# A hybrid decoder layer on one core: branch-weight sums formed in place in four load buffers from the head's second column group on, and a paced inverse that ends 480 matmuls from the last

## Chip, core and metric

One NeuronCore of one Trainium2 chip runs the whole layer in one launch. The metric is the device time of one execution in microseconds (us); the time before is the median of three runs. Engines are named as the profile names them: PE (TensorE matmul), PEld (its weight load), DVE (VectorE), ACT (ScalarE), POOL (GpSimd) and SP (SyncE, which here only issues DMAs, in order). `L123` is line 123 of the kernel before.

## What is computed

A decoder layer on 1024 rows of 1024 channels, float32 in and out:

```
hn   = rmsnorm(x);  proj = hn @ w_in
y_fox = forgetting_attention(fq, fk, fv, log_sigmoid(ff + bias))      # 8 heads of 128
y_gdn = gated_delta_rule(l2norm(q), l2norm(k), v, g, beta)            # q,k,v = silu(causal conv), chunks of 64
        # each chunk solves (I + A) sol = [v*beta, k*beta*exp(gc)], A strictly lower triangular 64x64
y = sigmoid(gate_fox) * (y_fox @ w_branch_fox) + sigmoid(gate_gdn) * (y_gdn @ w_branch_gdn)
h = x + y @ w_out
h = h + (silu(u_gate) * u_val) @ w_down,   u = causal conv(rmsnorm(h) @ w_up)
out = rmsnorm(h)
```

## The kernel before

Every float32 product is made of three matmuls on split operands (a high part in fp32r, copied by ACT, and the rest, subtracted by DVE or POOL: `split`, L106 and L107). Large products are done by Strassen's scheme in Winograd's form on 512-wide quarters: seven products of 12 matmuls in place of eight, with sums of quarters formed ahead (`weight_sums` for weights, `block_sums` for activations). The stages follow each other on PE in program order, since PE's order is written by hand; the other engines' orders are laid out by the framework's scheduler ahead of the run, and each engine, SP's DMA issues among them, runs its own list strictly in order.

**The head** (`head_in`, L541 on) normalises and transposes x, and multiplies it by the token weights `w_tok` in four column groups g of 262 columns and eight row tiles t: `rows(g, t)` is 24 matmuls into one of eight PSUM banks, an ACT copy into `vev` (two buffers, L574) and a DMA `vd<-vev` (L580). The group's weights come in quarters `vwr` (L560), are split by ACT and POOL into `vwh` and `vwl`, and have two buffers. Between the rows of the groups g = 1 to 3 the program also takes steps of two other generators: `scalars` (the gates' scalars) and `prepare_merge`, called `sums` there. `block_sums` forms the activation sums t1 to t4 of the next stage (DVE L343 to L362).

`prepare_merge` (L991) works ahead for a stage 1000 us later: for both branches and k = 0 to 3, eight blocks in all, it loads two 128x1024 tiles `raw` of `w_branch` (L1001, 512 KB each, two buffers), has DVE form four sums of 128x512 from their halves (L985 to L988, `weight_sums`), and stores them to DRAM (L1006, 1 MB). The sums go into a tile `sums` of 128x2048 with one buffer, so the next block's sums wait until this block's store has landed. One step issues a block's loads, the next its sums and its store; the loop in `head_in` takes one step for each row tile from g = 1, t = 4 on.

**The projections** (`project`, L716 on) follow: `strassen` runs 32 jobs of 84 matmuls (L156), 2688 in all; a job loads two weight tiles `wr` (L125, three buffers), forms the weight sums `ws` on DVE (L202), operands on ACT and POOL (`oh`, `ol`), and takes its results out of PSUM with ACT (`x`, L258; `c`, L311) and DVE (L289, L300, L315). Their buffers lie in memory that the head gives back. `left` counts the matmuls still to come, and the loop at L877 on uses it to thread other work between them:

- `inverse` (L922), the triangular solve of all chunks, 124 steps, nearly all of them a pair of DVE operations (L962, L964) on up to 128x512. It starts once the heads' own work is done, at `left = begin`, and is paced by one line:

```
if (begin - left) * INVERSE_STEPS >= (begin - 340) * steps:
```

- `prepare_lead` (L1009) in the memory that the inverse gives back, a step at each multiple of 20 of `left`: it loads six `w_up` tiles (L1017), forms one set of weight sums, splits 13 quarters into `parts` (two buffers) and stores them (L1023, `lead`) for the up projection.
- `fox_first` (L1072) in the memory that `prepare_lead` gives back: its first step loads the first attention head's q, k, v and bias rows (L1042, L1065); the later ones, at each multiple of 10 of `left` below 130, scale q (L1050), split k (`kh`, `kl`) and multiply (L1104 to L1106), the first time at `left` = 100.

**The merge** (`merge_block`, L1354) later loads the stored sums in 128x512 pieces (L1361).

Of the kernel before, what the change touches and what calls it, by code (L numbers as in the profile page):

```python
# [17 lines left out]
P = 128  # L18
# [69 lines left out]
class Block:  # L88
# [452 lines left out]
    def head_in(self, blk, right):  # L541
# [3 lines left out]
        with tc.tile_pool(name="hin", bufs=1) as pool, ExitStack() as px:  # L545
# [75 lines left out]
            for g in range(1, NVG):  # L621
                w = wgroup(g, nc.gpsimd)
                take(scalars, 1)
                for t in range(NT):
                    rows(g, t, *w)
                    if g > 1 or t > 3:
                        take(sums, 1)
                    if t % 4 == 2 and g < 3:
                        sl = slice((2 * (g - 1) + t // 4) * P, (2 * (g - 1) + t // 4 + 1) * P)
                        self.block_sums(blk, whole("12", sl), whole("22", sl), sl, pool)  # L630
# [85 lines left out]
    def project(self, blk, fox_pool):  # L716
# [159 lines left out]
        with ExitStack() as ix:  # L876
            for i, _ in enumerate(self.strassen(jobs, blk, pace=3)):  # L877
# [21 lines left out]
                elif prep is None:  # L899

                    if (begin - left) * INVERSE_STEPS >= (begin - 340) * steps:
                        steps += 1
                        if not take(inv, 1):
                            ix.close()
                            prep = self.prepare_lead(ix.enter_context(tc.tile_pool(name="prep", bufs=1, reuse_waits="tile")))
# [73 lines left out]

    def weight_sums(self, pool, a11, a12, a21, a22):  # L980

        v = self.nc.vector
        t = pool.tile([P, 2048], F32, tag="sums", bufs=1, name="sums")
        s1, s2, s3, s4 = (t[:, 512 * i:512 * (i + 1)] for i in range(4))
        self.tc.keep_in_program_order(v.tensor_tensor(s1, a21, a22, ALU.add))  # L985
        v.tensor_tensor(s2, s1, a11, ALU.subtract)
        v.tensor_tensor(s3, a11, a21, ALU.subtract)
        v.tensor_tensor(s4, a12, s2, ALU.subtract)  # L988
        return t

    def prepare_merge(self, pool):  # L991

        nc, a = self.nc, self.a
        self.ms_d = [[self.dr.tile([P, 2048], F32, name=f"ms{br}{k}") for k in range(4)] for br in range(2)]
        left, right = slice(0, 512), slice(512, 1024)
        for br in range(2):
            for k in range(4):
                raws = []
                for half in range(2):
                    t = pool.tile([P, 1024], F32, tag="raw", bufs=2, name="raw")  # L1000
                    self.tc.keep_in_program_order(nc.sync.dma_start(t, a["w_branch"][KD * br + 4 * half + k]))  # L1001
                    raws.append(t)
                yield
                r0, r1 = raws
                t = self.weight_sums(pool, r0[:, left], r1[:, left], r0[:, right], r1[:, right])
                self.tc.keep_in_program_order(nc.sync.dma_start(self.ms_d[br][k], t))  # L1006
                yield

    def prepare_lead(self, pool):  # L1009
# [10 lines left out]
        def parts(j, src):  # L1020
            t = pool.tile([P, 1024], F32R, tag="parts", bufs=2, name="parts")
            self.split(t[:, left], t[:, right], src)
            nc.sync.dma_start(self.lead_d[j], t.bitcast(F32))  # L1023

        w1, w2 = (load(a["w_up"][2 * FF_ORDER[0] + i]) for i in range(2))
        yield
        t = self.weight_sums(pool, w1[:, left], w1[:, right], w2[:, left], w2[:, right])
        parts(0, w1[:, left])
        parts(1, w1[:, right])
        yield  # L1030
        for i, n in enumerate((1, 2, 0, 3)):
            parts(9 + i, t[:, 512 * n:512 * (n + 1)])
        for j in range(1, 5):
# [320 lines left out]
    def merge_block(self, pool, br, name, k, t=None):  # L1354
# [4 lines left out]
        if name[0] == "s":  # L1359
            i = int(name[1]) - 1  # L1360
            self.nc.sync.dma_start(t, self.ms_d[br][k][:, 512 * i:512 * (i + 1)])  # L1361
            return t
# [569 lines left out]
```

## Time and profile before

| quantity | value |
|---|---|
| median of 3 runs | 2057.82 us (2057.77 to 2064.13) |
| the profiled execution | 2060.05 us, span 2058.3 us |
| mean granted TensorE clock | 0.978 |
| busy PE / DVE / ACT / POOL | 94% / 71% / 52% / 47% of the span |
| head, up to the first matmul of the projections | 166.08 us |
| projections' matmuls (L156) | 166.08 to 858.2 us |

The span runs from the first to the last instruction, and the profiled execution's own time is 1.75 us longer. A busy share of 94% on PE says that most stages are bound by it, and that what is to be won lies where it stands still. The profile's page cuts the span into 40 slices of 51.5 us and gives each engine's busy share in tenths; the stretches are then looked at one by one. In the views "[4.7 <-DMA x]" behind a row is the idle time of its engine just before it and what ended it, and "waited for" rows give the total, the times and the longest.

### The profile page before, as it was taken

The numbers are of one execution on the slowest core, as the hardware profiler recorded it, in microseconds if no ns is written. First come the engines' busy times: TensorE is split into PE (matmuls) and PEld (weight loads), VectorE is DVE, ScalarE is ACT, GpSimd is POOL, SyncE is SP. The second block draws the span as 40 slices with busy tenths as digits, with TensorE's granted clock in tenths as the row PEclk, the third lists the DMA queues.
The fourth block names the chain that finished last, engine by engine and source line by source line (L and its number), as shares of the span: only waits on it lengthen the run. The fifth ranks groups of instructions, "written<-read, shape, count | busy, mean of one in ns | idle before, by whom it ended". The sixth has DMA issues, their size and how long they took to land. (4 is left out here: it accounts for less than half of the span.)

```text
span 2058.3 us, 29148 instructions
## 1 busy us (share of the span) xinstructions
PE 1924.9 (94%) x9628; PEld 1605.7 (78%) x9628; DVE 1465.4 (71%) x2514; ACT 1076.3 (52%) x2354; POOL 973.2 (47%) x818
## 2 busy tenths in 40 slices
PE   7937999999999999788999999999999999999998
PEld 6935888878887787578887788777788888877886
DVE  8925776874898977466776898667867667677535
ACT  5304777764334445466767444366655555553224
POOL 5704556555555454346765333235565665640012
PEclk9968999999999999889999999999999999999999
DMA  4473444445333348557663863565443343368654
GB/s 161 141 250 121 139 131 149 141 138 193 109 113 118 108 143 301 199 182 234 196 224 112 307 197 116 175 210 184 134 145 117 128 142 119 128 216 324 222 194 159
DMA packets 177896, 350.95 MB, mean 171 GB/s; under 512 B 50320, under 2 KB 62928, under 8 KB 176720
## 3 DMA queue, kind: packets, MB, share of 16 engines
q1 hardware_dynamic: 177600, 348.56, 50.8%
q8 instruction: 76, 1.25, 0.3%
q14 instruction: 76, 0.62, 0.1%
q10 hardware_dynamic: 144, 0.52, 0.1%
HBM read 232.79 MB, written 116.23 MB: 170 GB/s over the span
## 5 line engine op out<-in xcount | busy, mean ns | idle before, releaser
L107 POOL TENSOR_TENSOR ol<-ws,oh 128x512 fp32r<-128x512 f32 x212 | 285.5, 1350 | 235.4 <-ACT oh L106 227.6
L107 POOL TENSOR_TENSOR ol<-wr,oh 128x512 fp32r<-128x512 f32 x165 | 231.6, 1405 | 313.5 <-ACT oh L106 213.4
L106 ACT CAST oh<-ws 128x512 fp32r<-128x512 f32 x212 | 130.9, 618 | 171.8 <-PE mm L156 163.7
L106 ACT CAST oh<-wr 128x512 fp32r<-128x512 f32 x204 | 123.5, 616 | 147.2 <-PE mm L156 80.1
L202 DVE TENSOR_TENSOR ws<-wr 128x512 f32<-128x512 f32 x106 | 97.8, 922 | 142.6 <-DMA wr<-in_w_up_dram 74.2
L377 DVE SCALAR_TENSOR_TENSOR cv<-c,fw,cv 128x512 f32<-128x512 f32 (+2 forms) x176 | 127.3, 748 | 16.5 <-ACT cv L372 15.3
L156 PE MATMUL mm<-b11h,oh 128*128 128x512 f32 x216 | 85.9, 398 | 42.2 <-ACT oh L106 42.2
L377 DVE SCALAR_TENSOR_TENSOR cv<-c,cw,cv 128x511 f32<-128x511 f32 (+2 forms) x144 | 105.9, 748 | 7.3 <-ACT cv L372 5.4
L962 DVE TENSOR_TENSOR invt<-invz 128x399 f32<-128x399 f32 (+50 forms) x114 | 95.7, 856 | 0.4
L156 PE MATMUL mm<-b22h,oh 128*128 128x512 f32 x216 | 86.7, 401 | 8.5 <-ACT x L258 8.2
L258 ACT COPY x<-mm 128x512 f32<-128x512 f32 x158 | 91.9, 582 | 4.5 <-PE mm L156 4.5
L156 PE MATMUL mm<-bt1h,oh 128*128 128x512 f32 x216 | 85.2, 394 | 4.8 <-ACT x L258 4.7
L107 DVE TENSOR_TENSOR ol<-wd,oh 128x512 fp32r<-128x512 f32 x66 | 46.3, 705 | 58.0 <-ACT oh L106 58.0
L156 PE MATMUL mm<-b22l,oh 128*128 128x512 f32 x216 | 86.5, 400 | 0.0
L156 PE MATMUL mm<-b11l,oh 128*128 128x512 f32 x216 | 86.1, 399 | 0.0
L156 PE MATMUL mm<-b11h,ol 128*128 128x512 f32 x216 | 86.0, 398 | 0.1
L156 PE MATMUL mm<-b21l,oh 128*128 128x512 f32 x216 | 86.0, 398 | 0.0
L156 PE MATMUL mm<-bt4l,oh 128*128 128x512 f32 x216 | 85.7, 397 | 0.0
L156 PE MATMUL mm<-bt2l,oh 128*128 128x512 f32 x216 | 85.1, 394 | 0.3 <-DVE bt2l L107 0.3
L156 PE MATMUL mm<-b22h,ol 128*128 128x512 f32 x216 | 85.1, 394 | 0.0
L156 PE MATMUL mm<-bt1l,oh 128*128 128x512 f32 x216 | 84.9, 393 | 0.0
L156 PE MATMUL mm<-bt3l,oh 128*128 128x512 f32 x216 | 84.8, 392 | 0.0
(404 smaller groups left out, 6388.4 us busy)
## 6 DMA issues: line engine op xcount, KB each, us to landing
wr<-in_w_up_dram SPq DMA_DIRECT2D x43, 512.0 KB, 3.7
wr<-in_w_gdn_dram SPq DMA_DIRECT2D x24, 512.0 KB, 3.6
wr<-in_w_out_dram SPq DMA_DIRECT2D x24, 512.0 KB, 4.4
s<-hy SPq DMA_DIRECT2D x44, 256.0 KB, 2.9
s<-z SPq DMA_DIRECT2D x44, 256.0 KB, 3.4
wd<-in_w_down_dram SPq DMA_DIRECT2D x44, 256.0 KB, 5.9
b22h<-s SPq DMA_DIRECT2D x44, 256.0 KB, 2.8
b22l<-s SPq DMA_DIRECT2D x44, 256.0 KB, 3.3
```

Of the source, the lines that this page charges most:

```text
L106: nc.scalar.copy(hi, src)
L107: (lo_eng or nc.vector).tensor_tensor(lo, src, hi.bitcast(F32), ALU.subtract)
L156: self.nc.tensor.matmul(ps, lhs[:, sl], rhs[:, k, :], start=(first and k == 0 and i == 0), stop=(k == 3 and i == 2), skip_group_check=True)
L202: v.tensor_tensor(t, x, y, op)
L258: nc.scalar.copy(t, x)
L377: nc.vector.scalar_tensor_tensor(t[:, lo:], c[:, 512 * j + lo - s:512 * (j + 1) - s], w[:, n - 1 - s:n - s], t[:, lo:], op0=ALU.mult, op1= ...
L962: nc.vector.tensor_tensor(tv, z[:, m:n, 0:n].to_broadcast([P, r, n]), z[:, m, c0:c1].unsqueeze(2).to_broadcast([P, r, n]), ALU.mult))
```

## The change

1. `weight_sums` writes its four sums into the halves that it read (in place) and needs no `sums` tile; `raw` in `prepare_merge` has four buffers in place of two, and each of a block's two `raw` tiles is stored by a DMA of its own (512 KB) into a tile of its own.
2. The loop in `head_in` takes a step of `sums` for every row tile from g = 1, t = 0 on, four row tiles earlier.
3. The inverse's pace ends at 480 matmuls from the last in place of 340.
4. `prepare_lead` uses the sums in place too (the two plain quarters are split first), and `parts` has four buffers in place of two.
5. `merge_block` finds each sum at its new place.

```diff
-                    if g > 1 or t > 3:
-                        take(sums, 1)
+                    take(sums, 1)
...
-                    if (begin - left) * INVERSE_STEPS >= (begin - 340) * steps:
+                    if (begin - left) * INVERSE_STEPS >= (begin - 480) * steps:
...
-    def weight_sums(self, pool, a11, a12, a21, a22):
+    def weight_sums(self, a11, a12, a21, a22):
 
         v = self.nc.vector
-        t = pool.tile([P, 2048], F32, tag="sums", bufs=1, name="sums")
-        s1, s2, s3, s4 = (t[:, 512 * i:512 * (i + 1)] for i in range(4))
-        self.tc.keep_in_program_order(v.tensor_tensor(s1, a21, a22, ALU.add))
-        v.tensor_tensor(s2, s1, a11, ALU.subtract)
-        v.tensor_tensor(s3, a11, a21, ALU.subtract)
-        v.tensor_tensor(s4, a12, s2, ALU.subtract)
-        return t
+        self.tc.keep_in_program_order(v.tensor_tensor(a22, a21, a22, ALU.add))
+        v.tensor_tensor(a21, a11, a21, ALU.subtract)
+        v.tensor_tensor(a11, a22, a11, ALU.subtract)
+        v.tensor_tensor(a12, a12, a11, ALU.subtract)
...
-                    t = pool.tile([P, 1024], F32, tag="raw", bufs=2, name="raw")
+                    t = pool.tile([P, 1024], F32, tag="raw", bufs=4, name="raw")
...
-                t = self.weight_sums(pool, r0[:, left], r1[:, left], r0[:, right], r1[:, right])
-                self.tc.keep_in_program_order(nc.sync.dma_start(self.ms_d[br][k], t))
+                self.weight_sums(r0[:, left], r1[:, left], r0[:, right], r1[:, right])
+                for d, t in zip(self.ms_d[br][k], raws):
+                    self.tc.keep_in_program_order(nc.sync.dma_start(d, t))
...
-            t = pool.tile([P, 1024], F32R, tag="parts", bufs=2, name="parts")
+            t = pool.tile([P, 1024], F32R, tag="parts", bufs=4, name="parts")
...
-        t = self.weight_sums(pool, w1[:, left], w1[:, right], w2[:, left], w2[:, right])
         parts(0, w1[:, left])
         parts(1, w1[:, right])
         yield
-        for i, n in enumerate((1, 2, 0, 3)):
-            parts(9 + i, t[:, 512 * n:512 * (n + 1)])
+        self.weight_sums(w1[:, left], w1[:, right], w2[:, left], w2[:, right])
+        for j, t in enumerate((w1[:, left], w2[:, left], w2[:, right], w1[:, right])):
+            parts(9 + j, t)
...
-            i = int(name[1]) - 1
-            self.nc.sync.dma_start(t, self.ms_d[br][k][:, 512 * i:512 * (i + 1)])
+            i, j = {"s2": (0, 0), "s3": (0, 1), "s4": (1, 0), "s1": (1, 1)}[name]
+            self.nc.sync.dma_start(t, self.ms_d[br][k][i][:, 512 * j:512 * (j + 1)])
```

The lines of the kernel after lie one to three above those before. SP's list shows the head's part. Where `prepare_merge` begins, before the change, SP has (numbers behind an underscore tell buffers and DRAM tiles apart; `ms00` is block 0's store):

```order
L580 DMA vd_91<-vev_807 128x262
L1001 DMA raw_818<-in_w_branch_dram 128x1024
L1001 DMA raw_820<-in_w_branch_dram 128x1024
L580 DMA vd_91<-vev_847 128x262
L580 DMA vd_91<-vev_881 128x262
L1001 DMA raw_884<-in_w_branch_dram 128x1024
L1006 DMA ms00_810<-sums_850 128x2048
L1001 DMA raw_886<-in_w_branch_dram 128x1024
```

And with the change (`ms000` and `ms001` are block 0's two stores, `raw_692` and `raw_694` its tiles):

```order
L580 DMA vd_91<-vev_673 128x262
L998 DMA raw_692<-in_w_branch_dram 128x1024
L998 DMA raw_694<-in_w_branch_dram 128x1024
L560 DMA vwr_1329<-in_w_tok_dram 128x524
L580 DMA vd_91<-vev_721 128x262
L560 DMA vwr_1333<-in_w_tok_dram 128x524
L580 DMA vd_91<-vev_755 128x262
L998 DMA raw_758<-in_w_branch_dram 128x1024
L998 DMA raw_760<-in_w_branch_dram 128x1024
L580 DMA vd_91<-vev_809 128x262
L1004 DMA ms000_676<-raw_692 128x1024
L560 DMA vwr_1337<-in_w_tok_dram 128x524
```

The first loads stand four `vd` rows earlier, block 1's loads stand ahead of block 0's stores, and two `vwr` loads of the third group's weights now stand behind branch-weight loads.

Where the head's list ends and the projections' loads `wr` begin, SP has before the change:

```order
L1001 DMA raw_1351<-in_w_branch_dram 128x1024
L1006 DMA ms11_815<-sums_1293 128x2048
L1001 DMA raw_1353<-in_w_branch_dram 128x1024
L580 DMA vd_91<-vev_1564 128x262
L1001 DMA raw_1417<-in_w_branch_dram 128x1024
L1006 DMA ms12_816<-sums_1383 128x2048
L1001 DMA raw_1419<-in_w_branch_dram 128x1024
L1006 DMA ms13_817<-sums_1449 128x2048
L125 DMA wr_1686<-in_w_gdn_dram 128x1024
```

And with it:

```order
L998 DMA raw_1269<-in_w_branch_dram 128x1024
L580 DMA vd_91<-vev_1432 128x262
L1004 DMA ms120_688<-raw_1201 128x1024
L580 DMA vd_91<-vev_1460 128x262
L1004 DMA ms121_689<-raw_1203 128x1024
L580 DMA vd_91<-vev_1488 128x262
L1004 DMA ms130_690<-raw_1267 128x1024
L1004 DMA ms131_691<-raw_1269 128x1024
L580 DMA vd_91<-vev_1516 128x262
L580 DMA vd_91<-vev_1544 128x262
L580 DMA vd_91<-vev_1572 128x262
L125 DMA wr_1694<-in_w_gdn_dram 128x1024
```

In both, the first `wr` stands behind the last block's store; with the change three of the last group's `vd` rows stand between them, where before the last `vd` came four rows ahead of the end.

The third place is SP's list around the first attention loads (`ql`), before the change (`gzd0` to `gzd7` are the results of the last eight chunks of the projections, two a job):

```order
L774 DMA gzd2_1655<-c1_7759 128x1024
L1023 DMA lead4_7552<-parts_7741 128x1024
L1023 DMA lead5_7553<-parts_7745 128x1024
L774 DMA gzd3_1656<-c2_7869 128x1024
L1023 DMA lead6_7554<-parts_7796 128x1024
L1023 DMA lead7_7555<-parts_7800 128x1024
L1023 DMA lead8_7556<-parts_7837 128x1024
L1042 DMA ql_7846<-qd0_1637 128x1024
```

And with it:

```order
L1021 DMA lead6_7318<-parts_7544 128x1024
L1021 DMA lead7_7319<-parts_7548 128x1024
L1021 DMA lead8_7320<-parts_7593 128x1024
L125 DMA wr_7819<-in_w_gz_dram 128x1024
L125 DMA wr_7821<-in_w_gz_dram 128x1024
L1040 DMA ql_7602<-qd0_1645 128x1024
L1040 DMA kl_7604<-kd0_1653 128x1024
L1063 DMA cr_7605<-rows_620 128x1024
L1040 DMA vl_7607<-vd_91 128x8x128
L773 DMA gzd0_1661<-c1_7645 128x1024
```

The attention loads stood behind `gzd3` and stand ahead of `gzd0` now, two jobs of the projections earlier.

More of the change, by code (lines that the diff above doesn't have):

```diff
@@ L977, in inverse @@
         self.dump("yd", self.y_d)
-    def weight_sums(self, pool, a11, a12, a21, a22):
+    def weight_sums(self, a11, a12, a21, a22):
         v = self.nc.vector
-        t = pool.tile([P, 2048], F32, tag="sums", bufs=1, name="sums")
-        s1, s2, s3, s4 = (t[:, 512 * i:512 * (i + 1)] for i in range(4))
-        self.tc.keep_in_program_order(v.tensor_tensor(s1, a21, a22, ALU.add))
-        v.tensor_tensor(s2, s1, a11, ALU.subtract)
-        v.tensor_tensor(s3, a11, a21, ALU.subtract)
-        v.tensor_tensor(s4, a12, s2, ALU.subtract)
-        return t
+        self.tc.keep_in_program_order(v.tensor_tensor(a22, a21, a22, ALU.add))
+        v.tensor_tensor(a21, a11, a21, ALU.subtract)
+        v.tensor_tensor(a11, a22, a11, ALU.subtract)
+        v.tensor_tensor(a12, a12, a11, ALU.subtract)
     def prepare_merge(self, pool):
         nc, a = self.nc, self.a
-        self.ms_d = [[self.dr.tile([P, 2048], F32, name=f"ms{br}{k}") for k in range(4)] for br in range(2)]
+        self.ms_d = [[[self.dr.tile([P, 1024], F32, name=f"ms{br}{k}{i}") for i in range(2)] for k in range(4)]
+                     for br in range(2)]
         left, right = slice(0, 512), slice(512, 1024)
```

## The prediction

> **What bounds it now.** I read the page's slices first, to find where PE stands still, then the waits, windows and rows of those places.
>
> ```profile
> span 2058.3 us, 29148 instructions
> PE   7937999999999999788999999999999999999998
> PEclk9968999999999999889999999999999999999999
> ```
>
> PE is full nearly everywhere. The third to fifth digits (103 to 206 us: 3, then 7) and the two at 823 to 926 us (7, 8) are the low ones, and the granted clock falls at the same places. The list of what PE waited for has two long rows, the first from 40 to 260 us, the second from 450 to 960 us; the windows and rows below belong to the first.
>
> ```profile
> PE mm L156 <- ACT oh L106: 42.2, 1, 42.2
> PE ms L1104 <- ACT kh L106: 7.3, 1, 7.3
> ...
> 124.00:166.00 42.00, 0.00 (x0) 0.00 (x0) 11.07 (x16) 2.66 (x8) 0.00 (x0) 0.53 0.69 245
> 160.00:175.00 15.00, 8.79 (x29) 6.68 (x30) 4.42 (x5) 5.55 (x12) 7.62 (x7) 0.65 0.59 211
> ...
> 107.54 0.69 DVE L988 TENSOR_TENSOR sums<-raw,sums 128x512 f32<-128x512 f32 x1
> 135.57 0.69 DVE L987 TENSOR_TENSOR sums<-raw 128x512 f32<-128x512 f32 x1 [6.68 <-DMA ms<-sums]
> 138.12 0.69 DVE L988 TENSOR_TENSOR sums<-raw,sums 128x512 f32<-128x512 f32 x1
> 145.65 0.69 DVE L987 TENSOR_TENSOR sums<-raw 128x512 f32<-128x512 f32 x1 [6.83 <-DMA ms<-sums]
> 157.96 0.32 SPq L1006 DMA_DIRECT2D ms<-sums  x1
> 161.84 1.28 SPq L125 DMA_DIRECT2D wr<-in_w_gdn_dram  x3
> 166.08 0.80 PE L156 MATMUL mm<-b11h,oh 128*128 128x512 f32 x1 [42.15 <-ACT oh L106]
> ```
>
> For 42 us PE does nothing because the first `wr` load stands on SP behind the last branch-weight store. That store is the end of a chain in which each block waits for the store of the one before: 145.65 - 135.57 = 10.1 us a block, of which about 7 are the wait for the store, with DVE, ACT and POOL nearly idle. From the last store's issue to the first matmul pass 166.08 - 157.96 = 8.1 us.
>
> **Term 1, the head.** With four tiles and no `sums`, two blocks are in flight, and a tile's round is load, sums, store, next load. Their lengths, from the DMA view of 96 to 162 us (GB/s in 40 slices; issues with KB each, median us from issue to landing):
>
> ```profile
> GB/s 0 7 273 439 328 373 13 111 258 417 251 295 225 27 121 313 432 397 232 75 86 375 441 397 222 0 119 271 442 402 201 0 112 390 432 338 0 0 397 238
> DMA packets 4897, 15.59 MB, mean 236 GB/s; under 512 B 544, under 2 KB 2464, under 8 KB 4000
> ...
> ms<-sums SPq DMA_DIRECT2D x7, 1024.0 KB, 6.3
> raw<-in_w_branch_dram SPq DMA_DIRECT2D x12, 512.0 KB, 5.4
> ...
> wr<-in_w_gdn_dram SPq DMA_DIRECT2D x1, 512.0 KB, 3.5
> ...
> 99.24 0.69 DVE L362 TENSOR_TENSOR tt<-tt,b21l 128x512 f32<-128x512 f32 x1
> ```
>
> A half-size store has no row; it lies between the 3.5 of the quickest half-size transfer and the 6.3 of the whole one. I take 6.3, since two halves leave together and move the same bytes. The round is 5.4 + 2.9 (four sums of 0.69 with their gaps, the last begun at 138.12 where the first could begin at 135.57, less a wait of 0.4) + 6.3 + 0.7 (two SP issues ahead) = 15.3 us for two blocks. The start: SP now loads blocks 0 and 1 ahead of any store, and DVE's list has block 2's sums around the last `block_sums` operation, the row of 99.24 before. Three sums more stand ahead of that row than before, so block 2 ends at 99.9 + 3 x 1.2 (between 0.69 and the 1.7 of sums beside a busy POOL) = 103.5, where it ended at 108.2 before; block 3, in the other two tiles, 3.5 later, at 107. Blocks 5 and 7 follow a round each: 107 + 2 x 15.3 = 137.6. The tail of 8.1 stays: three `vd` rows stand there now, but they are short beside it and one of them waits as `wr` did for the store. PE resumes at **145.7 instead of 166.1: 20.4 us less.** The bytes allow it: four blocks' loads and six blocks' stores, 10.5 MB, and 1.8 of `vd`, in 34 us are 360 GB/s, above the mean of 236, which holds pauses, and below the 380 of the row at 780 us.
>
> ```profile
> 780.00:790.00 10.00, 10.00 (x46) 8.29 (x45) 8.62 (x10) 5.50 (x10) 5.19 (x5) 1.00 1.02 380
> ```
>
> Bounds: rounds of 3.5 + 2.9 + 3.5 give 107 + 19.8 + 8.1 = 135 (31 less); rounds of 20, as slow a block as now, give 155 (11 less). PE idles for over 10 us in all of them, so the half clock of its first matmuls stays. The Trainium skill, "DMA: Bandwidth & Descriptors", section "Bandwidth", asks for transfers of 1 MiB or more, so it speaks against halving the stores. By its 341 GB/s at 1 MB against 138 at 64 KB a 512 KB store would be the poorer, and as an estimate from that page 1 to 2 us a block would go, 6 to 12 us of this term. The `raw` rows speak for less: 512 KB land in 5.4 where 1 MB needs 6.3, two at a time.
>
> ```profile
> 94.14 1.33 POOL L107 TENSOR_TENSOR vwl<-vwr,vwh 128x524 fp32r<-128x524 f32 x1
> 98.20 0.28 PE L570 MATMUL ms<-vwh,b21h 128*128 128x262 f32 x1
> ```
>
> The third group's last `vwl` split stands behind the last `block_sums` split on POOL now; it ends near 107 instead of 95.5, while PE reaches that group's later rows from 98.2 on. PE may lose up to 6 us there. It costs nothing: the wait until 145.7 lies behind it.
>
> **Term 2, the attention inputs.** At 821.6 us PE has 100 matmuls left and waits for the first attention head's k.
>
> ```profile
> 816.59 5.09 SPq L1023 DMA_DIRECT2D lead<-parts  x3
> 821.73 0.42 SPq L1042 DMA_DIRECT2D ql<-qd  x1
> ...
> 827.01 1.06 ACT L1050 ACTIVATE qh<-ql 128x1024 fp32r<-128x1024 f32 x1 [5.40 <-DMA ql<-qd]
> ...
> 773.16 3.01 SPq L1017 DMA_DIRECT2D raw<-in_w_up_dram x4
> ...
> ACT parts L106 <- DMA lead<-parts: 4.0, 5, 2.5
> ...
> 828.87 0.58 PE L1104 MATMUL ms<-kh,qh 128*128 128x256 f32 x1 [7.30 <-ACT kh L106]
> 511.90:755.40 243.50, 239.79 (x1053) 196.88 (x1052) 218.92 (x317) 95.18 (x166) 127.53 (x91) 1.00 0.34 114
> 820.00:830.00 10.00, 2.15 (x8) 1.24 (x7) 2.61 (x3) 3.81 (x6) 2.37 (x2) 0.79 0.87 284
> 830.00:840.00 10.00, 9.50 (x33) 7.93 (x34) 2.94 (x14) 4.91 (x12) 5.32 (x5) 0.70 0.03 8
> ```
>
> The loads stand behind the last `lead` store, and `prepare_lead` runs from 773.2 to 821.7, as it starts when the inverse is out of its memory. Ending the inverse 140 matmuls earlier moves all that by 140 x 0.2277 (239.79 / 1053, the row of 511.90) = 31.9 us against PE; the loads and splits need 828.87 - 821.73 = 7.1 of them, which leaves 24 us. The four `parts` add the 4.0 of ACT's waits. Gone: 7.3 of waiting, 1.0 of the next, and the clock: 0.3 of the 9.5 busy us at 830 to 840 and 0.5 of the 1.1 before, 3.4. **11.7 us less.** Bounds 8 (a remainder at POOL, where `kl` and `cd` now stand ahead of nine operand splits) and 12.
>
> **Term 3, the denser inverse.** Its window is the row of 511.90 above, in which 124 steps end at 340 matmuls from the last. DVE's groups in it (busy, mean ns | idle before):
>
> ```profile
> L962 DVE TENSOR_TENSOR invt<-invz 128x399 f32<-128x399 f32 (+50 forms) x114 | 95.7, 856 | 0.4
> L964 DVE TENSOR_TENSOR invz<-invz,invt 128x399 f32<-128x399 f32 (+50 forms) x114 | 61.0, 547 | 1.7
> ...
> L202 DVE TENSOR_TENSOR ws<-ws,wr 128x512 f32<-128x512 f32 x13 | 13.2, 1019 | 6.8 <-POOL ol L107 6.7
> L300 DVE TENSOR_TENSOR c<-mm,x 128x512 f32<-128x512 f32 x13 | 8.9, 687 | 10.5 <-ACT x L258 10.5
> ```
>
> 1053 matmuls pass for 114 pairs, 9.2 each; 124 steps put the start near 340 + 124 x 9.3 = 1490 left, and the new end makes the stretch (1490 - 480) / (1490 - 340) = 0.88 as long, 214 us. DVE is busy for 218.9 us; the groups add up to 235 (they overlap), 156.7 of it the inverse, so 145.8 busy us are its own and 73 the projections', 0.30 a us. Afterwards: 145.8 + 0.30 x 214 = 210 of 214 us, 98% where it was 90%. PE loses 3.7 us in this window now (243.5 - 239.79). At best DVE's idle time, which is waiting for work, simply goes, and PE loses nothing more. At worst all 24.6 us of it stay, shortened to 21.6, on top: 210 + 21.6 - 214 = 17.6 more. I take **4 us more**, twice the present loss, the nearest row.
>
> The merge's 128x512 loads keep their bytes and their stage; I cost them at 0, within 1 either way, hidden by their four to six buffers.
>
> **Sum.** -20.4 - 11.7 + 4.0 = -28.1, from the profiled execution's 2060.05: 2032. That execution is 2.2 above the median, so against 2057.82 the forecast is **2030 us**. PE sets the pace between these places, so what is won in the head arrives at the end.
>
> **Rivals.**
> - *The chain keeps up with the rows.* With short transfers PE resumes at 135 or before: 31 less, 2019. For it: slices above 400 GB/s in the GB/s row; against: SP's list puts loads behind stores that wait for DVE.
> - *The overlap is not had.* SP is in order, and a load waiting for its tile's store holds up all behind it. At 10 us a block PE resumes at 155: 2039.
> - *The attention wait stays,* because DVE and ACT, busy with the inverse, finish `prepare_lead` as late as now: 2042.
> - *Slower.* DVE becomes the bound from 500 to 730 us. L962 has a median of 682 ns and a longest of 1806:
>
> ```profile
> L962 DVE TENSOR_TENSOR invt<-invz x114: 186/682/1806, 511.9 to 755.3; 128x504 f32<-128x504 f32 x10, 128x510 f32<-128x510 f32 x8, 128x495 f32<-128x495 f32 x5, 128x494 f32<-128x494 f32 x5
> ```
>
>   If more of them meet a busy POOL, PE waits for DVE's results. With 4 us in hand it loses 114 x (mean - 0.856) - 4; the 32 us that would eat terms 1 and 2 need a mean of 1.17 us, and every one at 1.806 would cost 104 (2130). POOL's 91 operations in the window do not grow, which speaks against it. The Trainium skill, "SBUF — State Buffer", section "Who interferes with whom", has a DVE operation with two SBUF inputs and a reading GpSimd operation block each other fully, which is this rival's mechanism. The longest row against the median, 1.1 us more, agrees with it.
>
> **How the numbers follow.** Forecast (PE back at 138 to 152, attention wait gone, inverse 0 to 10): 55%, 2022 to 2041. Quick chain 15% (2012 to 2022), no overlap 15% (2036 to 2044), attention wait stays 7% (2042), inverse at its worst bound 5% (2044), slower 3%. The range 2013 to 2044 leaves out an end of each side case, under 2 in 10. A measurement of this kernel tells about 0.3%, 6 us, from no change: faster by more 0.94, within 0.03, slower 0.03.
>
> **What would show it.** Right: the wait `mm L156 <- ACT oh` near 20 us or under and its matmul near 146; raw loads landing in 5 to 6 us with no DVE wait for a store; no row `L1104 <- ACT kh`; `ql` issued some 30 us ahead of need; DVE at 95% or more in the inverse's window and PE's loss there 4 to 11. Wrong: DVE waiting for `raw` for 10 us a block, or PE waiting for `ACT x` or `DVE c` by tens of us between 490 and 700.

## The result and the profile after

The changed kernel takes **2031.39 us** (median of 4 runs, 2028.34 to 2033.09) where the kernel before takes 2057.80 (2055.75 to 2064.13, 4 runs): a ratio of 0.9865, 95% interval 0.9839 to 0.989. The forecast was 2030, within 2013 to 2044. The profiled execution took 2033.09 us, 27.0 less than the one of before.

The page's slices of the kernel after, the same three rows as of before:

```profile
span 2031.3 us, 29170 instructions
PE   7869999999999999898999899999999999999998
PEclk9979999999999999899999999999999999999999
```

The low digits near the start, the second and third now, are 8 and 6 where the third and fourth were 3 and 7, and behind the sixteenth only scattered 8s are left. What PE waited for, the longest rows (engine, line, releaser: us in total, times, longest):

```profile
PE mm L156 <- ACT x L258: 13.9, 16, 2.0
PE mm L156 <- ACT oh L106: 12.9, 1, 12.9
...
PE ms L700 <- DVE rt L688: 8.0, 1, 8.0
```

The wait of 42.2 us is 12.9 now, the 7.3 for `kh` are gone, and a wait of 8.0 in the head is new (`rt`, below). To see where each microsecond went I follow the projections' matmuls, the first 2688 of line L156, which are the same in the same order in every kernel here. The table has the start of the first, the time from it to the 1249th (about where the inverse begins), on to the 2521st (the inverse), on to the 2605th (the job in which the attention begins) and on to the span's end:

```
                     first   to 1249th  to 2521st  to 2605th  to the end   span
before               166.1     345.8      293.6      32.0      1220.9     2058.3
after                143.2     346.8      299.9      19.8      1221.7     2031.3
difference           -22.9      +1.0       +6.3     -12.2        +0.8      -27.0
forecast             -20.4         0       +4.0     -11.7           0      -28.1
```

**The head.** DVE's rows of the kernel after where the chain ends (start, us, engine, line, operation, tiles; in brackets the idle time before and what ended it), the median landing of a `raw` load from 96 to 143 us, SP's rows, and PE's first matmul of the projections:

```profile
111.92 0.69 DVE L982 TENSOR_TENSOR raw<-raw 128x512 f32<-128x512 f32 x1 [7.07 <-issue]
115.58 0.69 DVE L982 TENSOR_TENSOR raw<-raw 128x512 f32<-128x512 f32 x1 [0.79 <-DMA raw<-in_w_branch_dram]
...
127.02 0.69 DVE L982 TENSOR_TENSOR raw<-raw 128x512 f32<-128x512 f32 x1 [8.49 <-DMA raw<-in_w_branch_dram]
```
```profile
raw<-in_w_branch_dram SPq DMA_DIRECT2D x8, 512.0 KB, 4.9
```
```profile
132.65 1.05 SPq L1004 DMA_DIRECT2D ms<-raw  x2
133.74 4.27 SPq L580 DMA_DIRECT2D vd<-vev  x3
138.10 1.35 SPq L125 DMA_DIRECT2D wr<-in_w_gdn_dram  x3
```
```profile
143.15 0.80 PE L156 MATMUL mm<-b11h,oh 128*128 128x512 f32 x1 [12.95 <-ACT oh L106]
```

Blocks come in pairs now, 127.02 - 111.92 = 15.1 us a pair where one block took 10.1. DVE waits for loads, no longer for a store. The last store leaves at 133.4 (the second of the pair of 132.65); behind it, three `vd` rows take 4.3 us of SP before the first `wr` load.

**The inverse.** Its window in the kernel after (PE, PEld, DVE, ACT, POOL busy with counts, granted clock, DMA share, GB/s), and DVE's rows just ahead of its longest wait:

```profile
489.90:709.40 219.50, 212.87 (x924) 173.83 (x924) 208.65 (x307) 81.63 (x143) 113.42 (x80) 0.99 0.32 110
```
```profile
548.83 1.79 DVE L202 TENSOR_TENSOR ws<-wr,ws 128x512 f32<-128x512 f32 x1
550.54 0.67 DVE L963 TENSOR_TENSOR invz<-invz,invt 128x504 f32<-128x504 f32 x1
551.13 0.57 DVE L961 TENSOR_TENSOR invt<-invz 128x399 f32<-128x399 f32 x1
551.73 0.57 DVE L963 TENSOR_TENSOR invz<-invz,invt 128x399 f32<-128x399 f32 x1
552.22 0.68 DVE L300 TENSOR_TENSOR c<-mm,x 128x512 f32<-128x512 f32 x1
```
```profile
548.37 0.58 ACT L258 COPY x<-mm 128x512 f32<-128x512 f32 x1
```
```profile
552.95 0.80 PE L156 MATMUL mm<-bt4h,oh 128*128 128x512 f32 x1 [2.26 <-DVE c L300]
```

DVE is busy for 208.65 of 219.5 us, 95%. The result operation L300 had its input from ACT at 548.95, stood in DVE's list behind a sum of 1.79 us and three operations of the inverse, and began at 552.22; PE, waiting for its bank, stood still for 2.26 us. What PE waited for from 480 to 760 us, before and after:

```profile
PE mm L156 <- ACT x L258: 3.6, 4, 1.6
```
```profile
PE mm L156 <- ACT x L258: 4.4, 5, 1.5
PE mm L156 <- DVE c L300: 2.7, 2, 2.3
```

So of the 6.3 us that the stage is longer, 3.5 are waits, most of them on DVE. Another 1.7 go to a lower clock behind the longest wait (in the last section), and the last microsecond isn't traced.

**The attention inputs.** SP issues them at 767.44, 38 us ahead of need, and PE goes from the projections into the attention without a wait:

```profile
767.44 0.47 SPq L1040 DMA_DIRECT2D ql<-qd  x1
...
805.05 0.39 PE L156 MATMUL mm<-b11l,oh 128*128 128x512 f32 x1
805.27 0.28 PE L1102 MATMUL ms<-kh,qh 128*128 128x256 f32 x1
```

### The profile page after: what moved, and what is told of

It reads as the page before. It is cut to its first block, busy times and chain, and to the rows that moved or that the text cites. A ratio compares the mean times of both kernels' runs of the same rounds, so it can differ in the third digit from the quotient of the medians.

```text
span 2031.3 us, 29170 instructions
## 1 busy us (share of the span) xinstructions
PE 1924.7 (95%) x9628; PEld 1605.3 (79%) x9628; DVE 1468.3 (72%) x2514; ACT 1076.7 (53%) x2354; POOL 976.6 (48%) x818
## 5 line engine op out<-in xcount | busy, mean ns | idle before, releaser
L202 DVE TENSOR_TENSOR ws<-wr 128x512 f32<-128x512 f32 x106 | 106.7, 1007 | 152.1 <-DMA wr<-in_w_up_dram 73.3
L156 PE MATMUL mm<-b11h,oh 128*128 128x512 f32 x216 | 85.6, 396 | 12.9 <-ACT oh L106 12.9
L961 DVE TENSOR_TENSOR invt<-invz 128x399 f32<-128x399 f32 (+50 forms) x114 | 94.8, 846 | 0.4
L156 PE MATMUL mm<-b22h,oh 128*128 128x512 f32 x216 | 85.9, 398 | 8.2 <-ACT x L258 8.2
L156 PE MATMUL mm<-bt1h,oh 128*128 128x512 f32 x216 | 85.2, 395 | 5.8 <-ACT x L258 5.7
L156 PE MATMUL mm<-bt4h,oh 128*128 128x512 f32 x216 | 85.5, 396 | 2.7 <-DVE c L300 2.7
L156 PE MATMUL mm<-bt4l,oh 128*128 128x512 f32 x216 | 86.3, 399 | 0.0
L156 PE MATMUL mm<-b22l,oh 128*128 128x512 f32 x216 | 86.1, 398 | 0.0
L156 PE MATMUL mm<-b21l,oh 128*128 128x512 f32 x216 | 86.0, 398 | 0.0
L156 PE MATMUL mm<-b11l,oh 128*128 128x512 f32 x216 | 85.7, 397 | 0.0
L156 PE MATMUL mm<-b11h,ol 128*128 128x512 f32 x216 | 85.3, 395 | 0.1
L156 PE MATMUL mm<-bt2l,oh 128*128 128x512 f32 x216 | 85.1, 394 | 0.3 <-DVE bt2l L107 0.3
L156 PE MATMUL mm<-bt1l,oh 128*128 128x512 f32 x216 | 84.9, 393 | 0.0
L156 PE MATMUL mm<-bt4h,ol 128*128 128x512 f32 x216 | 84.8, 392 | 0.0
```

The costliest lines, as they stand in the source:

```text
L156: self.nc.tensor.matmul(ps, lhs[:, sl], rhs[:, k, :], start=(first and k == 0 and i == 0), stop=(k == 3 and i == 2), skip_group_check=True)
L202: v.tensor_tensor(t, x, y, op)
L961: nc.vector.tensor_tensor(tv, z[:, m:n, 0:n].to_broadcast([P, r, n]), z[:, m, c0:c1].unsqueeze(2).to_broadcast([P, r, n]), ALU.mult))
```

## The experiments

Twelve kernels, each beside runs of the kernel before on its chip. The profiled executions by the stages of the table above, with the median and the ratio to before with its interval:

```
                     first  to 1249th to 2521st to 2605th to the end  median   ratio (95%)
pace_only            165.7    346.2    301.0     19.8     1217.4     2053.63  0.9976 (0.9961 to 0.9991)
head_only            144.2    347.1    293.6     24.1     1218.7     2029.57  0.9865 (0.9847 to 0.9882)
late_start           148.7    346.9    300.5     19.8     1215.7     2037.03  0.9905 (0.988 to 0.993)
early_only           158.2    345.3    293.6     31.5     1219.1     2050.28  0.9973 (0.9955 to 0.9991)
pace_380             143.2    346.8    292.6     19.8     1221.6     2024.39  0.9824 (0.9803 to 0.9846)
early5               141.6    345.7    299.8     19.8     1220.6     2028.66  0.9849 (0.9832 to 0.9866)
two_raw              166.8    347.7    299.3     19.8     1218.1     2054.21  0.9981 (0.9967 to 0.9995)
one_store            146.3    346.2    299.9     19.8     1220.9     2035.87  0.9887 (0.9863 to 0.9911)
parts2_340           144.3    345.4    293.6     31.0     1220.9     2037.57  0.9905 (0.9887 to 0.9924)
late_rt_380          145.1    346.6    293.7     19.8     1214.1     2021.69  0.9825 (0.9806 to 0.9845)
early5_late_rt_380   142.0    345.0    291.3     19.8     1213.8     2017.34  0.9803 (0.9783 to 0.9823)
early5_vd_act_380    156.9    346.7    291.3     19.8     1216.6     2032.63  0.9857 (0.9828 to 0.9886)
```

The stages up to the 2605th matmul repeat within 1 to 2 us where nothing in them was changed. In the first stage part of that comes from its very start: the rows of the first column group, which most of the edits don't touch, end anywhere from 49.2 to 51.1 us. The rest behind the 2605th, which no experiment touches, lies anywhere from 1213.8 to 1221.7, so a difference of a few microseconds in a median says little, and the verdicts below rest on the stages.

### The change taken apart: pace_only, head_only, late_start, early_only

**pace_only**, the kernel before with one number changed:

```diff
-                    if (begin - left) * INVERSE_STEPS >= (begin - 340) * steps:
+                    if (begin - left) * INVERSE_STEPS >= (begin - 480) * steps:
```

> The kernel before with the pace's end alone, 480 for 340. Theory (terms 2 and 3 stand by themselves): the wait of 7.3 us for kh goes with the 1.05 and the half clock behind it, 12 us, and the denser inverse takes 4 to 7 back, so 5 to 8 us less than before, about 2051, with PE still resuming near 166. Rival (prepare_lead's own four buffers are what frees the attention inputs): the wait for kh stays at 4 us or more, and the time is 2058 or above.

The attention job falls to 19.8 us and the inverse's stage grows by 7.4 (4 to 7 expected): 0.9976, 5 us less than before, as the theory had it. `prepare_lead`'s buffers are not needed for this gain.

**head_only**, the kernel after with 340 put back:

```diff
-                    if (begin - left) * INVERSE_STEPS >= (begin - 480) * steps:
+                    if (begin - left) * INVERSE_STEPS >= (begin - 340) * steps:
```

> The kernel after with the pace's end at 340 as before. Theory (terms add): 23 us less than before from the head, PE resuming near 143, and the wait for kh 3 to 7.3 us since parts has four buffers; 2031 to 2036. Rival (the head's gain is partly given back later): PE resumes near 143 but the time is 2040 or above.

The time is under the range expected, and level with the kernel after. The head's part is as expected, but the waits for k are 1.0 and 1.2 us, not 3 to 7.3, and the attention job takes 24.1 us. The waits of PE from 755 to 850 us in head_only, and SP's rows of `prepare_lead` there:

```profile
PE ms L1103 <- POOL kl L107: 1.2, 1, 1.2
PE ms L1102 <- ACT kh L106: 1.0, 1, 1.0
```
```profile
752.99 2.72 SPq L1015 DMA_DIRECT2D raw<-in_w_up_dram  x4
...
792.17 0.42 SPq L1040 DMA_DIRECT2D ql<-qd  x1
```

From the first load to `ql` it takes 39.2 us, where the kernel before took 821.73 - 773.16 = 48.6. That is 9.4 us, more than the wait it had to remove. So with the new `prepare_lead` the pace at 480 buys 4.3 us (24.1 to 19.8) and costs 6.3 in the inverse. The two parts of the change are not additive: alone against before they save 5 and 28 us by their ratios, together 28.

**late_start**, the kernel after with the old first step, and **early_only**, the kernel before with the new one:

```diff
# late_start, against the kernel after
-                    take(sums, 1)
+                    if g > 1 or t > 3:
+                        take(sums, 1)
```

> The kernel after with the first step of the branch-weight sums at row tile 4 of the second group, as before. The first load moved by 13.2 us (71.8 to 58.5), and the chain from first load to last store shrank from 86.2 to 74.8 us, 11.4. Theory (both parts count, each by its own): PE resumes 12 to 14 us later than in the kernel after, near 156, and the time is about 2044. Rival (the buffers alone do it, as DVE's list around the block sums at 99 us sets block 2 whenever the loads begin): within 4 us of the kernel after, 2031 to 2035.

> The kernel before with the first step of the branch-weight sums four row tiles earlier, alone: one buffer of sums, 1 MB stores, two raw buffers. Theory (both parts count): the chain keeps its 10 us a block and starts 13 us earlier, PE resumes near 153, time about 2045. Rival (block 2's sums stay where DVE's list has them, near 100 us, so nothing behind them moves): PE resumes at 160 or later, 2052 or above.

Both expectations missed. The early start is worth 148.7 - 143.2 = 5.5 us on top of the buffers and 166.1 - 158.2 = 7.9 without them, where 12 to 14 were expected; the buffers are worth 17.4 (late_start against before) or 15.0. Of the 5.5 and the 17.4 about 0.9 is uncertain, since late_start's first group of rows, which the edit doesn't touch, ends at 50.1 for 49.2. Part of what is missing stands in SP's rows of the kernel after, above: there the last store left at 133.4, but the last three `vd` stores held the first `wr` until 138.10, 4.7 us behind the store. In late_start the last `vd` was gone at 136.0, the last store left at 142.5 and `wr` at 144.5, 2.0 behind it. So the `vd` stores cost some 2.7 us.

### Pace, buffers and store size: pace_380, early5, two_raw, one_store

**pace_380** is the kernel after with 380 for 480.

> The kernel after with the pace's end at 380. At 340 (head_only) the attention loads left SP at 135 matmuls from the last, 35 before their use, and PE still lost 4.3 us more in that job than in the kernel after; up to that job the kernel after had lost 6.1 us more to the inverse. Theory (the inverse's price is steep only when DVE is nearly full, and 40 matmuls of lead are enough): the job before the attention takes under 21 us, the inverse costs under 2 us against 340, time 2026 to 2028. Rival (the price is linear in the pace and the kh wait needs the whole lead): the inverse costs 2 us or more against 340 and the job takes over 22, time 2029 to 2031.

The theory holds, and more than that (2024.39 is under its range): the attention job is as short as with 480, and the inverse costs nothing against 340. Its window (the row has the columns of the inverse's row above) and PE's waits for DVE from 480 to 760 us:

```profile
491.20:722.00 230.80, 228.38 (x1003) 187.46 (x1002) 215.06 (x312) 89.53 (x156) 119.21 (x87) 1.00 0.33 113
```
```profile
PE mm L156 <- DVE c L300: 1.1, 1, 1.1
```

PE loses 2.4 us there with DVE 93% busy; the kernel after lost 6.6 at 95%, the kernel before 3.7 at 90%. The loss doesn't simply rise with DVE's share: it is a handful of single waits, and the pace also moves which operations of the inverse stand ahead of a result on DVE. The six kernels with 480 all have the wait of 2.26 us (2.27 in late_start); none of the others has it. All four runs (2018.83 to 2026.03) lie under all four of the kernel after.

**early5** begins the sums in the first column group:

```diff
+            sums = self.prepare_merge(pool)
             for t in range(NT):
...
                     rows(0, t - 1, *w0)
+                if t >= 5:
+                    take(sums, 1)
...
-            sums = self.prepare_merge(pool)
             for g in range(1, NVG):
```

> The kernel after with the branch-weight sums begun three row tiles earlier still, in the first column group (from t = 5). Theory (the chain is still what ends last in the head; of the 13 us of earlier start between late_start and the kernel after, 5.6 arrived): PE resumes at 135 to 140, 3 to 8 us less, time 2024 to 2028. Rival (the earlier loads take the DMA and SP's list from the token weights, the rows of the first and second group come late, and nothing arrives): PE resumes at 142 or later, 2031 or above.

The first load leaves 21 us earlier than in the kernel after, and PE resumes 1.5 us earlier, at 141.6: the rival's "142 or later" is nearer than the theory. Its reason isn't settled: the rows of the first two groups end at 51.2 and 74.6 us, 2.0 later than in the kernel after, but late_rt_380 below, without the earlier start, has 51.1 and 74.5. What PE waited for in early5 up to 145 us:

```profile
PE mm L156 <- ACT oh L106: 7.6, 1, 7.6
PE ms L702 <- DVE rt L690: 7.1, 1, 7.1
```

The last rows end at 134.0 in place of 130.2, the last store leaves at 130.2, and the wait behind the rows is 7.6 us. The rows and their `vd` stores, not the chain, end last here.

**two_raw** leaves everything of the change but the two further buffers:

```diff
-                    t = pool.tile([P, 1024], F32, tag="raw", bufs=4, name="raw")
+                    t = pool.tile([P, 1024], F32, tag="raw", bufs=2, name="raw")
```

> The kernel after with two raw buffers in prepare_merge in place of four: sums in place, half-size stores, early start, but no two blocks in flight. Theory (the overlap of two blocks is what shortens the chain): a block takes load 4.9 + sums 2.9 + store 3.1 to 6.3 + issues, 11 to 15 us, so the last store leaves near 58 + 8 x 13 = 162 and PE resumes at 155 to 178, time 2043 to 2066. Rival (the smaller stores shorten it, not the overlap): PE resumes before 150, time under 2038.

PE resumes at 166.78: the whole head gain is gone, early start included. DVE's rows in two_raw:

```profile
148.40 0.69 DVE L982 TENSOR_TENSOR raw<-raw 128x512 f32<-128x512 f32 x1 [8.49 <-DMA raw<-in_w_branch_dram]
159.40 0.69 DVE L982 TENSOR_TENSOR raw<-raw 128x512 f32<-128x512 f32 x1 [8.12 <-DMA raw<-in_w_branch_dram]
```

A block takes 11 us, one more than before, since its buffers are free only when its store has landed. In-place sums without more buffers are a loss per block; the pair in flight is the gain. The last store leaves at 162.3, later than before the change (158.0). PE resumes at the same time all the same, because SP's list is another here: the first `wr` loads leave at 121.51, long ahead of the last blocks. Yet PE waits, because ACT's first operand does, and that for the landing of the last store, not for a load:

```profile
166.11 1.14 ACT L106 CAST oh<-wr 128x512 fp32r<-128x512 f32 x2 [28.31 <-DMA ms<-raw]
```

So the chain holds the projections in two ways: through SP's list, which every kernel with `wr` behind the last store shows, and, here at least, through this landing, which holds them even with `wr` loaded.

**one_store** keeps both tiles of a block in one of 128x2048 and stores it whole:

```diff
-                    t = pool.tile([P, 1024], F32, tag="raw", bufs=4, name="raw")
+                whole = pool.tile([P, 2048], F32, tag="raw", bufs=2, name="raw")
...
+                    t = whole[:, 1024 * half:1024 * (half + 1)]
...
-                for d, t in zip(self.ms_d[br][k], raws):
-                    self.tc.keep_in_program_order(nc.sync.dma_start(d, t))
+                self.tc.keep_in_program_order(nc.sync.dma_start(self.ms_d[br][k], whole))
```

> The kernel after with a block's two halves in one tile of 128x2048 (two buffers) and one store of 1 MB. Theory (two half-size stores move the same bytes at the same rate, and the first can leave one sum earlier): PE resumes at 143 to 148, time 2031 to 2036. Rival (larger transfers are the cheaper ones, 1 to 2 us a block): PE resumes before 139, time under 2027.

PE resumes 3.1 us later; 0.9 of it stands in the first group's rows already (50.1 us for 49.2), so some 2 are left to the store, with a theory that holds. From 96 to 143 us the whole store lands in 4.4 us, the half-size one of the kernel after in 3.5, from the DMA view of each:

```profile
ms<-raw SPq DMA_DIRECT2D x6, 1024.0 KB, 4.4
```
```profile
ms<-raw SPq DMA_DIRECT2D x12, 512.0 KB, 3.5
```

The Trainium skill ("DMA: Bandwidth & Descriptors", section "Bandwidth") is right that the large transfer moves a byte more cheaply (4.4 us against 3.5 for twice the bytes), but the time goes the other way. By the program the whole store begins one sum later and frees nothing until all of it has landed; the trace also has the loads beside it landing in 6.0 us for 4.9. Which of these makes the 2 us wasn't tested.

### What shortened prepare_lead, and a better kernel: parts2_340, late_rt_380, early5_late_rt_380, early5_vd_act_380

**parts2_340** is head_only with two `parts` buffers for four.

> The kernel after with the pace's end at 340 and two parts buffers in prepare_lead, so that of the change to prepare_lead only the order (the two plain quarters first) and the sums in place are left. From the first w_up load to the first attention load it took 48.5 us in the kernel before, 46.5 in pace_only and 39.2 in head_only. Theory (the four buffers take the 7 to 9 us off): 45 us or more here, the attention loads leave SP with under 115 matmuls left, PE loses 8 to 12 us in that job, time 2033 to 2038. Rival (the order does it: PE's splits begin ahead of the sums): 41 us or less, time 2028 to 2031.

The theory holds: 47.8 us from the first load (751.56) to `ql` (799.40), and the wait is back. PE's wait in parts2_340:

```profile
PE ms L1102 <- ACT kh L106: 7.4, 1, 7.4
```

So the four buffers take 47.8 - 39.2 = 8.6 us off `prepare_lead`. The new order's 0.8 is too little to tell: the old `prepare_lead` itself took 48.6 us in the kernel before and 46.5 in pace_only.

**late_rt_380** has the pace at 380 and takes the step of `scalars` that makes PE wait for `rt` later, **early5_late_rt_380** has early5's start as well:

```diff
-                take(scalars, 1)
+                if g < 3:
+                    take(scalars, 1)
                 for t in range(NT):
                     rows(g, t, *w)
+                    if g == 3 and t == 3:
+                        take(scalars, 1)
```

> The pace's end at 380, and the third step of scalars (the transposition of rt, for which PE stood still 8.0 us in the kernel after, at 96 us) taken behind the fourth row tile of the last group. Theory (the last rows end 8 us earlier and their vd stores no longer stand between the last branch-weight store and the first wr load): PE resumes at 138 to 140, 3 to 5 us before pace_380, time 2019 to 2022. Rival (the chain of branch weights alone sets the end): PE resumes at 142 to 144, time 2023 to 2026.

> The same with the branch-weight sums begun in the first column group (t = 5). In early5 the last store left at 130.2 but the last rows ended at 134.0, so the rows had become the bound. Theory (rows and chain both end earlier now): PE resumes at 131 to 137, time 2013 to 2019. Rival (the DMA is full from 100 us on, and the chain does not get shorter by an earlier start): PE resumes at 139 or later, time 2020 or above.

In the head both theories fall: the wait for `rt` is gone, but PE resumes at 145.1 and 142.0, no sooner than the rivals had it. In late_rt_380 the rows end at 129.7 all the same: two other waits of 2.0 and 2.7 us came in its place, and its rows run 1.9 us late from the first group on (51.1 for 49.2). In early5_late_rt_380 they end at 125.4 and the last store leaves at 130.1, yet `wr` must wait; SP's rows there:

```profile
129.41 1.05 SPq L1009 DMA_DIRECT2D ms<-raw  x2
...
132.33 4.75 SPq L580 DMA_DIRECT2D vd<-vev  x4
137.17 1.35 SPq L125 DMA_DIRECT2D wr<-in_w_gdn_dram  x3
```

`vev` has two buffers, so each of these `vd` stores waits for an ACT copy, which waits for an earlier `vd` to land. This is a second chain, and PE's rows hardly move its end: they end at 125.4 here, at 130.2 in the kernel after and at 134.0 in early5, and the last `vd` leaves SP at 137.1, 138.0 and 137.1, `wr` right behind it. Once the branch weights were faster than that, neither an earlier start nor earlier rows could bring much. The times are nevertheless the two lowest, 2021.69 and **2017.34 us**; that both lie in the theories' ranges is luck, as the next figures show. By the stages, early5_late_rt_380 gains 1.2 us in the head, 3 between the head and the attention, and 8 behind the 2605th matmul against pace_380. The last, the largest, is in a part that the edit doesn't touch (5.7 of it between the 2605th matmul and the merge); where it comes from stays open. The kernel is faster than the one after (0.9783 to 0.9823 against 0.9839 to 0.989); that it is faster than pace_380 the intervals don't settle.

**early5_vd_act_380** lets ACT issue the `vd` stores:

```diff
-                nc.sync.dma_start(self.vd[t * P:(t + 1) * P, c0:c0 + VGW - lo], ev[:, lo:VGW])
+                (nc.scalar if g else nc.sync).dma_start(self.vd[t * P:(t + 1) * P, c0:c0 + VGW - lo], ev[:, lo:VGW])
```

> early5_late_rt_380 with the vd stores of the second to fourth column group issued by ACT, behind the copy into vev, in place of SP. There the last rows ended at 125.4 and the last branch-weight store left at 130.1, but the first wr load left only at 137.2, behind vd stores that waited on SP for vev (32.6 us in all from 60 us on). Theory (SP's order is now what holds the wr loads): the last branch-weight store leaves at 130 or before, wr within 1 us of it, PE resumes at 128 to 136, time 2003 to 2012. Rival (the bytes set it: the DMA is near 300 GB/s from 100 us on, and ACT now stands for vev's landings as SP did): PE resumes at 139 or later, time 2014 or above.

The theory falls: PE resumes at 156.9, 15 us later. That and the time lie where the rival had them, but not for its reason. `wr` does leave right behind the last stores; SP's rows show another order:

```profile
128.80 1.05 SPq L1009 DMA_DIRECT2D ms<-raw  x2
129.90 1.77 SPq L1003 DMA_DIRECT2D raw<-in_w_branch_dram  x2
...
139.15 1.05 SPq L1009 DMA_DIRECT2D ms<-raw  x2
140.25 1.76 SPq L1003 DMA_DIRECT2D raw<-in_w_branch_dram  x2
149.71 1.05 SPq L1009 DMA_DIRECT2D ms<-raw  x2
150.86 1.72 SPq L125 DMA_DIRECT2D wr<-in_w_gdn_dram  x2
```

Each block's loads now stand behind the stores of the block ahead, so that only one block is in flight, 139.15 - 128.80 = 10.4 us each, with four buffers there. With the `vd` rows gone the framework laid out SP's list this way; why, wasn't pursued. So what PE gains when no `vd` store stands ahead of `wr` remains untested. Buffers alone do not overlap two blocks: the list must have the next loads ahead of the stores.

## Why the prediction was right, point by point

- **Term 1, the head: 22.9 us for 20.4.** The mechanism was shown by two_raw (no gain without the second pair of buffers), by early5_vd_act_380 (one block at a time, with four buffers) and by late_start (17.4 of the 22.9 without the early start). The round of two blocks was forecast at 15.3 us and is 15.1, but in part by luck. The store was taken at the upper end, 6.3 us, and landed in 3.5; load, sums and store come to 4.9 + 2.9 + 3.5 = 11.3, and the remaining 3.8, by subtraction the issues and waits on SP, were taken as 0.7. Block 3's last sum ends at 104.9 for 107, and from there to block 7's, at 133.3, two rounds take 28.5 us for 30.6. So the chain's last store left at 133.4 against 137.6 forecast. The tail took 9.8 for the 8.1 that were to stay: the first `wr` left 4.7 us behind the last store for 3.9 before, and the first matmul came 5.1 behind `wr` for 4.2.
- **The three `vd` rows, called short, were not.** The prediction had them hidden beside the wait of the first `wr` for the last store. They hold it 4.7 us behind that store, where late_start, with the `vd` stores gone, needs 2.0: some 2.7 us. That lost time in the third group "costs nothing" agrees with the runs so far: PE lost 8.0 us there (for `rt`, not for POOL's split, which was priced at up to 6), and late_rt_380 without that wait resumed no sooner.
- **The bound "no overlap", 155, was wrong.** It let a block take 10 us as before, from an early start. early_only, which is that, resumed at 158.2; two_raw took 11 us a block and resumed at 166.8.
- **Term 2, the attention inputs: 12.2 us for 11.7.** Right in size and in its cause as forecast: pace_only has the same 19.8 us in that job. But it was mis-sized what the four `parts` buffers add: 4.0 were read from ACT's waits, and parts2_340 against head_only shows 8.6. That is nearly the whole need, so the job's wait is mostly gone without the new pace, which the prediction did not see. With two remedies for one wait the term could hardly come out much smaller; that it was right does not vouch for the share of either. (31.9 - 7.1 leaves 24.8 us there, not 24; nothing hangs on it.)
- **Term 3, the denser inverse: 6.3 us for 4.0.** Inside its bounds of 0 to 17.6, but the 4 was a guess, twice the loss of before. DVE came to 95% busy for the 98% forecast. Of the 6.3, 3.5 are more waiting, most of it for a result behind DVE's list, and 1.7 the lower clock behind the longest wait, which the term did not have. It is not the mechanism of the rival "slower": L961's mean is 846 ns (856 before), far from the 1.17 us that would have made it so.
- **The merge and the rest: +0.8 for 0.** From its first matmul to its last the merge takes 162.4 us before and 162.3 after (162.2 in one_store): the half-size blocks cost it nothing. The rest, 1220.9 and 1221.7, is far within its spread of 8 us.
- **The sum** of -28.1 is off by 1.1 because the misses cancel: -2.5 in the head, -0.5 in the attention, +1.0 and +2.3 before and in the inverse, +0.8 behind. So near a hit is luck; each term by itself was right to about 2.5 us.
- One reading ahead of the terms was off: the low digits near the start (3, then 7, 103 to 206 us) are the third and fourth, not the third to fifth.

## What to carry to other kernels

When a change has two remedies for one wait, price each with the other in place: here the buffers had already paid for most of what the denser pace was to buy, and 380 in place of 480 gave both gains for no cost. Two blocks are in flight only if there are buffers for two *and* the issuing engine's list has the second block's loads ahead of the first one's stores; look at both. Work that is threaded into another engine's slack is free up to a point only: of three paces of the inverse the two slower ones cost PE next to nothing against each other, the densest 6 to 7 us. Try more than one.

## What the runs showed of the hardware

A short wait of PE can cost more than itself. Around the wait of 2.26 us in the kernel after (PE, PEld, DVE, ACT, POOL, granted clock, DMA share, GB/s):

```profile
550.00:555.00 5.00, 2.74 (x9) 1.89 (x8) 4.97 (x9) 1.10 (x2) 1.62 (x2) 0.79 0.62 208
555.00:560.00 5.00, 5.00 (x21) 4.07 (x20) 5.00 (x9) 0.62 (x1) 1.60 (x1) 0.87 0.02 7
```

The granted clock is 0.79 and 0.87 in this stretch and the next, where it is 1.00 just before, so that some 1.7 us more are lost (0.21 and 0.13 of 5 us). In the kernel before, a wait of 1.57 us left it at 1.00, and so did the same wait of 2.26 us in two_raw:

```profile
620.00:625.00 5.00, 3.43 (x15) 2.51 (x14) 4.93 (x8) 2.14 (x4) 2.98 (x2) 1.00 0.01 3
```
```profile
575.00:580.00 5.00, 2.74 (x12) 1.94 (x12) 4.97 (x9) 1.10 (x2) 2.04 (x2) 1.00 0.51 178
```

The Trainium skill ("TensorE: Matmul & The Clock Gate", section "What's actually happening") has the clock fall after an idle window of about 3.4 us, counted in windows that run freely. Here less was enough, but not each time: of the six kernels with this wait the clock fell in five and not in two_raw, in pace_only it fell behind one of 1.96 us too, and in no kernel behind those of 1.57 or less in this stage. That a wait of the same length does both would fit windows that run freely; no run tests it.

An operation's size can tell little of its time on DVE while POOL works beside it. The additions of 128x8 into `carry` (L685), ahead of `rt` in the kernel after, take 0.18 us or 1.26, all three below while a subtraction of POOL runs; rows of DVE, and of POOL:

```profile
95.01 0.18 DVE L685 TENSOR_TENSOR carry<-carry,tot 128x8 f32<-128x8 f32 x1
96.30 1.26 DVE L685 TENSOR_TENSOR carry<-carry,tot 128x8 f32<-128x8 f32 x1
98.68 1.26 DVE L685 TENSOR_TENSOR carry<-carry,tot 128x8 f32<-128x8 f32 x1
```
```profile
93.69 3.83 POOL L107 TENSOR_TENSOR bt1l<-tt,bt1h 128x512 fp32r<-128x512 f32 x1 [1.28 <-ACT bt1h L106]
97.49 2.42 POOL L107 TENSOR_TENSOR bt2l<-tt,bt2h 128x512 fp32r<-128x512 f32 x1
```

The two long additions end at 97.56 and 99.94, within 0.04 us of the ends of POOL's subtractions (97.52 and 99.91): they end when POOL does. POOL's, in turn, take 3.83 and 2.42 us where 128x512 takes 1.35 and 1.40 in its two largest groups. The branch-weight sums of DVE stand among these rows and lengthen the way to `rt`, for which PE stood still for 8.0 us. It takes both parts of the change: with the early start alone PE waits 2.2 us for `rt` (early_only), with the buffers alone 1.5 (late_start), with the early start and two buffers 0.8 (two_raw). That POOL is what stretches the additions is read from these rows; no run tried the contention by itself.
